# Low parts of weights, the sum of decay directions, the modulation and two copies of k and v placed on VectorE

## The chip, the cores and the metric

The kernel runs on one core of a Trainium2 chip. The metric is the device time of one launch in microseconds (us); the time of a kernel is the median of its runs. Engines are named as the profile names them: PE (TensorE, matrix products), VectorE (DVE), ScalarE (ACT), GpSimd (POOL) and SyncE (SP, which only issues DMAs here). SBUF is the memory on the core that the engines work in, PSUM the one that PE's results land in.

## The reference: what is computed

Two layers of a backbone, for 128 context tokens and 512 latent tokens that share every weight; the kernel holds them as five token tiles of 128 (tile 0 is the context). Each layer is one adaLN sub-layer:

```python
h = rms_norm(x, norm_w) * (1 + scale) + shift      # scale, shift, gate from silu(cond) @ mod_w
x = x + gate * mixer(h)
```

Layer 0's mixer is gated grouped-query attention (16 heads, 4 key/value heads, head width 64) with QK-norm and axial rotary positions; latent queries also see 128 cached keys. Layer 1's mixer is a bidirectional state-space scan (SSD: 32 heads in 4 groups, state 128, chunks of 128 tokens): a projection, a centred convolution of width 3 on x, B and C, a softplus for the time steps, and per group and chunk

```python
decay  = exp(a_cs[l] - a_cs[s]) below the diagonal (forward), above it (backward)
y_diag = ((c @ b.T) * decay) @ x
state  = state * chunk_decay + b.T @ (x * decay_end);   y_off = (c @ state) * exp(a_cs)
y      = rms_norm((y_forward + y_backward + d_skip * x) * silu(z)) @ w_out
```

All inputs and outputs are float32. The kernel returns both token streams, the new keys and values, and the final states of the context.

## The kernel before

**Split products.** PE multiplies in a shorter format. To keep float32 accuracy every operand is split in a high part (a cast) and a low part (the source less the high part), and each product is three: high x high, high x low, low x high. `split` (L72 to L74) does that: ScalarE casts (L73), and the engine given, VectorE unless another is named, subtracts (L74). For weights, `load_split` fetches a raw piece of up to 1024 columns by DMA into one of two buffers ("raw"), rotates the list `weng` by one and gives its first engine to `split`; "wh" and "wl" are the two halves of the result, in two buffers each. So `weng` says who makes the low parts of weights: GpSimd for the first key/value weights, VectorE for the rest of these and for the first q weights (L331, L336), GpSimd alone in the rest of layer 0 and at the start of layer 1 (L690, L1020), VectorE, GpSimd, GpSimd in turn from the fourth x unit of layer 1 on (L1234), VectorE alone from the output projection of layer 1 on (L1217).

**Layer 0.** The x tiles are normalised, transposed and modulated; keys and values of all five tiles are projected together in four quarters (`mm_kv`, L379), and after the last quarter ScalarE copies each tile's sum out of PSUM into `kv` (L396). A key chain per tile follows: sum of squares (L469, L472), `rstd` on GpSimd, scaling (L476), rotation (L487 to L490). Then come, per key/value head, q projections (L283), q chains of the same kind, scores (L630), softmax (L633, L637), transposed probabilities that are split (names pt, ph, pl), P times V (L668) and the silu gate (L527 to L530), while the modulation of layer 1 is projected in the background (L175). The output projection (L841) adds the gated result to x: VectorE multiplies (L865) and adds (L866) in quarters of 256 columns.

**Layer 1's input.** Each finished tile is normalised (L877, name xn), transposed by PE in two halves (L242), and `h_half` (L244 to L253) modulates each half, four blocks of 128 channels x 128 tokens: one VectorE multiplication by scale from PSUM with the scale spread over the tokens (L251), one GpSimd addition of shift (L252), then the split.

**Time steps and units.** A *unit* is a projection of 128 channels over all tokens (L914, 48 matmuls into one of two PSUM buffers "pj") and its evacuation: for x, B and C a convolution by three VectorE steps out of PSUM (L1001 to L1003), a ScalarE tanh (L1005) and one more step (L1006); for z a ScalarE tanh (L1068) and a VectorE step (L1069). The time-step stage (`dt_stage`) runs between the first x units: a chain of some twenty small VectorE steps on 128x320 (L947 to L962; L956 is a series of seven), then cumulative sums by three matmuls (L966, L967, L972), ScalarE exponentials and a store to device memory from which the decay tables are loaded.

**SSD groups.** For each of the four groups and five tiles: `a_load` fetches the two directions' cumulative sums, each spread over all partitions as 128x1024 (names am; the forward one in two buffers, the backward one in one); `decay` masks them on GpSimd (L1126, L1127), takes 16 exponentials on ScalarE (L1131) and adds the backward to the forward one on GpSimd (L1132), by which the only backward buffer comes free for the next tile's load; `mix` multiplies with C x B out of PSUM on VectorE (L1138); `diag` multiplies with x on PE (L1145). Besides, per group: states (L1192 on PE, L1195 and L1196 on VectorE), the off-diagonal part (L1186 to L1188), the gating of Y by silu(z) (L1097 on VectorE), and the units of the next group. Layer 1's output projection (L1383) takes its weights in pieces of 1024 columns.

**What sets the order.** The Python code gives the program; at build time a scheduler (`schedule_with_timeline_sim=True`, L1476) places every engine's instructions in an order of its own from estimates of their time. On the chip each engine works through its list in that order, so an instruction whose input is late holds all that stand behind it.

## Time and profile before

| | |
|---|---|
| three runs | 992.88, 988.27, 991.97 us |
| median | 991.97 us |
| profiled execution, its own time | 996.43 us |
| its span in the profile | 994.6 us |
| PE busy | 933.1 us, 94% of the span |
| VectorE, ScalarE, GpSimd busy | 663.8, 517.4, 411.8 us |
| mean granted TensorE clock | 0.979 of full speed |
| moved by DMA | 146.98 MB, mean 148 GB/s |

The profile is one execution. An engine is "busy" while it executes an instruction; time in which it waits for another engine or a DMA is idle time, put down to what ended it. Matmuls are pipelined, so a busy PE is not a PE at its peak. The stages follow one another: set-up and key/value stage to about 110 us, attention to 375, output projection of layer 0 with the normalisation of layer 1 to 460, time steps and first x units to 500, the four groups to 860, output projection of layer 1 to the end.

### The profile page before, as it was taken

What the parts mean: (1) busy time and instruction counts of PE and PEld (TensorE: products, weight loads), DVE (VectorE), ACT (ScalarE), POOL (GpSimd) and SP (SyncE); (2) the same over time, 40 slices, a digit from 0 to 9 for tenths busy, and PEclk for the clock granted to TensorE, in tenths of its full rate; (3) what the DMA queues carried; (4) which work ended last, traced back from release to release, by engine and by line L of the source; (5) the groups of instructions that cost most, each with busy time, mean ns of one, the idle gap of its engine ahead of it and who ended that gap; (6) DMA issues with size and microseconds to landing.
All of it is one profiled execution on the core that took longest, in us unless ns stands there. A gap on an engine that the chain in (4) does not pass through costs nothing.

```text
span 994.6 us, 17413 instructions
## 1 busy us (share of the span) xinstructions
PE 933.1 (94%) x6578; PEld 845.7 (85%) x6578; DVE 663.8 (67%) x1046; ACT 517.4 (52%) x1208; POOL 411.8 (41%) x397
## 2 busy tenths in 40 slices
PE   5998999999999989989899989999999999989898
PEld 3887979979997779989799979799889899768686
DVE  4468666566675774884858776856686657898553
ACT  5345666667675763333446565456436552544340
POOL 3245235227271071364235676448543862332000
PEclk9899999999999999999999999999999999999899
DMA  9941253131114223333449766755476545456742
GB/s 307 348 143 50 84 165 128 47 103 36 29 44 128 85 66 109 124 107 89 128 139 264 199 197 198 183 181 157 155 206 189 183 132 160 145 180 206 256 161 101
DMA packets 121476, 146.98 MB, mean 148 GB/s; under 512 B 8688, under 2 KB 93808, under 8 KB 121392
## 3 DMA queue, kind: packets, MB, share of 16 engines
q1 hardware_dynamic: 110640, 140.62, 46.0%
q10 hardware_dynamic: 10752, 5.24, 1.8%
q8 instruction: 52, 0.85, 0.4%
q14 instruction: 32, 0.26, 0.1%
HBM read 128.73 MB, written 17.10 MB: 147 GB/s over the span
## 4 chain that ended last, share of the span: by engine, by line
PE 55%; DVE 16%; DMA 12%; issue 6%; POOL 5%; ACT 5%; SPq 1%; ACTq 0%; POOLq 0%; DVEq 0%
PE pj L914 15%; PE pp L283 8%; DMA am<-acd 5%; PE pj L1383 3%; PE po L668 3%; PE acc L379 3%; PE a L841 3%; PE S L630 3%; PE pt L658 3%; DVE wl L74 2%; DMA u<-yzd 2%; PE pp L175 2%; PE a L1383 2%; POOL am L1132 2%; PE a L1192 2%
## 5 line engine op out<-in xcount | busy, mean ns | idle before, releaser
L914 PE MATMUL pj<-h,wh 128*128 128x322 f32 (+1 forms) x1248 | 289.9, 319 | 10.0 <-DVE B L1006 4.5
L914 PEld LDWEIGHTS pj<-h,wh 128*128 128x128 f32 (+1 forms) x1248 | 210.8, 189 | 19.2 <-issue 12.0
L74 POOL TENSOR_TENSOR wl<-raw,wh 128x512 fp32r<-128x512 f32 (+1 forms) x70 | 134.9, 1938 | 178.7 <-ACT wh L73 178.4
L914 PE MATMUL pj<-h,wl 128*128 128x322 f32 (+1 forms) x624 | 200.6, 322 | 0.0
L73 ACT CAST wh<-raw 128x1024 fp32r<-128x1024 f32 (+1 forms) x117 | 103.2, 912 | 91.3 <-DMA raw<-in_l_w_out 27.9
L1131 ACT ACTIVATE am<-am,nb 128x128 f32<-128x128 f32 x320 | 98.1, 390 | 57.6 <-POOL am L1127 46.2
L914 PEld LDWEIGHTS pj<-h,wl 128*128 128x128 f32 (+1 forms) x624 | 118.4, 190 | 4.2 <-issue 3.8
L283 PE MATMUL pp<-wh,big 128*128 128x256 f32 x576 | 112.2, 285 | 0.5 <-ACT sg L527 0.5
L74 DVE TENSOR_TENSOR wl<-raw,wh 128x1024 fp32r<-128x1024 f32 x47 | 66.7, 1428 | 40.9 <-ACT wh L73 40.9
L283 PEld LDWEIGHTS pp<-wh,big 128*128 128x128 f32 x576 | 91.2, 188 | 0.9 <-ACT sg L527 0.7
L283 PE MATMUL pp<-wl,big 128*128 128x256 f32 x288 | 81.2, 282 | 0.0
L74 DVE TENSOR_TENSOR pl<-pt,ph 128x512 fp32r<-128x512 f32 (+1 forms) x100 | 59.2, 599 | 25.6 <-ACT ph L73 25.0
L633 DVE TENSOR_REDUCE nm<-S 128x1 f32<-128x640 f32 x64 | 52.4, 820 | 13.7 <-PE S L630 12.7
L73 ACT CAST ph<-pt 128x512 fp32r<-128x512 f32 (+1 forms) x100 | 51.4, 518 | 18.8 <-PE pt L658 14.1
L1132 POOL TENSOR_TENSOR am<-am,am 128x1024 f32<-128x1024 f32 x20 | 49.2, 2458 | 22.5 <-ACT am L1131 22.5
L637 ACT ACTIVATE Pt<-S,nm 128x640 f32<-128x640 f32 x64 | 51.3, 803 | 13.1 <-PE pt L658 9.5
L1383 PE MATMUL pj<-wh,h 128*128 128x512 f32 x160 | 54.0, 412 | 2.1 <-ACT wh L73 2.1
L283 PEld LDWEIGHTS pp<-wl,big 128*128 128x128 f32 x288 | 54.3, 188 | 0.0
L630 PE MATMUL S<-kT,qT 128*128 128x320 f32 x256 | 51.4, 326 | 2.3 <-ACT Pt L637 2.3
L658 PE MATMUL pt<-cst,Pt 128*128 128x128 f32 x320 | 50.7, 275 | 2.7 <-DVE pl L74 2.3
L1126 POOL TENSOR_SCALAR_AFFINE_SELECT am<-am 128x1024 f32<-128x1024 f32 x20 | 23.5, 1176 | 59.0 <-DMA am<-acd 51.5
L841 PE MATMUL a<-wh,big 128*128 128x256 f32 x256 | 46.8, 283 | 0.0
(345 smaller groups left out, 2114.9 us busy)
## 6 DMA issues: line engine op xcount, KB each, us to landing
raw<-in_l_w_in SPq DMA_DIRECT2D x48, 512.0 KB
am<-acd SPq DMA_DIRECT2D x40, 512.0 KB
raw<-in_l_w_out SPq DMA_DIRECT2D x36, 512.0 KB
og<-in_l_mod_w SPq DMA_DIRECT2D x29, 512.0 KB
E<-ecd SPq DMA_DIRECT2D x64, 128.0 KB
raw<-in_l_w_in SPq DMA_DIRECT2D x25, 256.0 KB
mw<-in_l_mod_w SPq DMA_DIRECT2D x11, 512.0 KB
ys<-dud SPq DMA_DIRECT2D x20, 256.0 KB
```

The costliest lines, as they stand in the source:

```text
L73: (heng.tensor_copy if heng else self.nc.scalar.copy)(hi, src)
L74: (eng or self.nc.vector).tensor_tensor(lo, src, r32(hi), op=ALU.subtract)
L283: nc.tensor.matmul(ps, a[:, k, cs], b[:, k, :], start=k == 0 and a is hi and b is w[0], stop=k == KD - 1 and a is lo)
L630: nc.tensor.matmul(S[:, 192 + 320 * q:512 + 320 * q], qTs[g, t][:, h, :], kT[:, hl, 320 * q:320 * q + 320], start=hl == 0, stop=hl == 1)
L633: nc.vector.tensor_reduce(c["m"], c["s"], axis=AX.X, op=ALU.max, negate=True)
L637: nc.scalar.activation(Pt, c["s"], AF.Exp, bias=c["m"], scale=1.0, accum_out=rss[g][t][:, h:h + 1])
L658: nc.tensor.transpose(pt[:, 2 * i + j, :], Pts[j][:, kt * P:kt * P + P], self.ident)
L841: self.nc.tensor.matmul(ps, self.ohl[a][:, k, ts], w[b][:, k, :], start=k == 0 and i == 0, stop=k == KD - 1 and i == 2)
L914: nc.tensor.matmul(ps[0:m, 190 + 322 * half:512 + 322 * half], w[b][:, k, off:off + m], hT[s][:, k, 322 * half:322 * half + 322], start=fi ...
L1131: nc.scalar.activation(af[d][:, h, :], af[d][:, h, :], AF.Exp, bias=self.nb[:, t, i:i + 1], scale=1.0)
L1132: nc.gpsimd.tensor_tensor(af[0], af[0], af[1], op=ALU.add)
L1383: nc.tensor.matmul(self.PS[t][n], y[a][:, kk, :], b, start=k0 + k == 0 and i == 0, stop=k0 + k == 15 and i == 2)
```

## The change

Four edits put work on VectorE, and nothing that is computed changes.

1. The copies out of PSUM of k and v for the last two tiles (t of 3 and 4) are made by VectorE; the first three stay on ScalarE.
2. `weng` is VectorE alone in all the program but the first key/value weights. 66 low parts of weights (33 of 128x1024 and 33 of 128x512) go from GpSimd to VectorE; 4 at the start stay on GpSimd.
3. The sum of the two decay directions (20 of 128x1024) goes from GpSimd to VectorE.
4. In `h_half`, ten times, the multiplication of 128x512 on VectorE and the addition on GpSimd become four VectorE instructions of 128x128, each of which multiplies by scale and adds shift.

```diff
-        nc.vector.tensor_tensor(m, src, self.scale[layer][:, k, c:c + 1].to_broadcast([P, 4, P]), op=ALU.mult)
-        nc.gpsimd.tensor_tensor(m, m, self.shift[layer][:, k, c:c + 1].to_broadcast([P, 4, P]), op=ALU.add)
+        for i in range(4):
+            k_ = 4 * half + i
+            nc.vector.tensor_scalar(out=m[:, i, :], in0=src[:, i, :], scalar1=self.scale[layer][:, k_, c:c + 1], scalar2=self.shift[layer][:, k_, c:c + 1], op0=ALU.mult, op1=ALU.add)
         self.split(hi[:, k, cs], lo[:, k, cs], m)
...
-                        nc.scalar.copy(self.kv[:, :, 5 if t == 0 else t, :], acc[t].rearrange("p (a n) -> p a n", a=2))
+                        (nc.scalar.copy if t < 3 else nc.vector.tensor_copy)(self.kv[:, :, 5 if t == 0 else t, :], acc[t].rearrange("p (a n) -> p a n", a=2))
...
-        self.weng = [nc.gpsimd]
+        self.weng = [nc.vector]
         order = [1, 2, 0, 3, 4]
...
     def layer1(self, hT, wp, pj, pa, ctx):
...
-        self.weng = [nc.gpsimd]
         wk = self.pool("s2", bufs=2, ctx=ctx)
...
-            nc.gpsimd.tensor_tensor(af[0], af[0], af[1], op=ALU.add)
+            nc.vector.tensor_tensor(af[0], af[0], af[1], op=ALU.add)
...
     def part_mm(k0):
-            self.weng = [nc.vector]
...
-        self.weng = [nc.vector, nc.gpsimd, nc.gpsimd]
```

The first edit adds a line, so from there to about L1018 the changed kernel's line numbers are one higher than those of the kernel before (L915 for L914). Because the scheduler places all instructions anew, their order changes beyond the four edits. Three places follow; in each row stand the line, the operation, output<-inputs with the program's buffer numbers, and the shape.

The first is VectorE at the end of the key/value stage, before the change (qss and qn belong to the key chains, acc is the PSUM sum of one tile):

```order
L472 TENSOR_REDUCE qss_809<-qsq_803 128x4
L476 TENSOR_TENSOR qn_805<-kv_82,qss_799 128x256
L472 TENSOR_REDUCE qss_821<-qsq_813 128x4
L476 TENSOR_TENSOR qn_815<-kv_82,qss_809 128x256
L74 TENSOR_TENSOR wl_787<-raw_789,wh_788 128x1024
```

and after it:

```order
L473 TENSOR_REDUCE qss_809<-qsq_803 128x4
L477 TENSOR_TENSOR qn_805<-kv_82,qss_799 128x256
L397 COPY kv_82<-acc_105 128x2x256
L473 TENSOR_REDUCE qss_821<-qsq_813 128x4
L397 COPY kv_82<-acc_106 128x2x256
L477 TENSOR_TENSOR qn_815<-kv_82,qss_809 128x256
L74 TENSOR_TENSOR wl_787<-raw_789,wh_788 128x1024
```

The two copies stand among the key chains of earlier tiles and ahead of the next low part.

The second is VectorE in the time steps, before the change (am and xs are the chain's values, u_6307 is the evacuation of the second x unit, u_6399 that of the third):

```order
L1001 TENSOR_SCALAR u_6307<-pj_6308,cw_556,cols_110 128x641
L956 SCALAR_TENSOR_TENSOR am_1330_6153<-am_1330_6153 128x320
L1002 SCALAR_TENSOR_TENSOR u_6307<-pj_6308,cw_556,u_6307 128x641
L957 SCALAR_TENSOR_TENSOR am_1330_6153<-am_1330_6153,am_1329_6152 128x320
L1003 SCALAR_TENSOR_TENSOR u_6307<-pj_6308,cw_556,u_6307 128x641
L958 SCALAR_TENSOR_TENSOR am_1330_6153<-am_1329_6152,am_1330_6153 128x320
L960 SCALAR_TENSOR_TENSOR am_1331_6154<-am_1330_6153,xs_6150 128x320
L962 TENSOR_SCALAR am_1331_6154<-am_1330_6153 128x320
L1006 SCALAR_TENSOR_TENSOR u_6307<-pj_6308,u_6307 128x641
```

and after it, where the second x unit is u_6327 and the third u_6419:

```order
L957 SCALAR_TENSOR_TENSOR am_1330_6173<-am_1330_6173 128x320 x2
L1007 SCALAR_TENSOR_TENSOR u_6327<-pj_6328,u_6327 128x641
L957 SCALAR_TENSOR_TENSOR am_1330_6173<-am_1330_6173 128x320
L1002 TENSOR_SCALAR u_6419<-pj_6420,cw_556,cols_110 128x641
...
L957 SCALAR_TENSOR_TENSOR am_1330_6173<-am_1330_6173 128x320 x2
L1007 SCALAR_TENSOR_TENSOR u_6419<-pj_6420,u_6419 128x641
L958 SCALAR_TENSOR_TENSOR am_1330_6173<-am_1330_6173,am_1329_6172 128x320
L959 SCALAR_TENSOR_TENSOR am_1330_6173<-am_1329_6172,am_1330_6173 128x320
L961 SCALAR_TENSOR_TENSOR am_1331_6174<-am_1330_6173,xs_6170 128x320
```

The chain's last steps stood inside the second unit's evacuation; now they stand behind the third's. On PE, the cumulative sums stood before the change inside the third unit (pj_6400):

```order
L914 MATMUL pj_6400<-h_1183_5264,wl_6389 128x322
L966 MATMUL a_6374<-am_1331_6154,xs_6150 128x5x32
L967 MATMUL a_6374<-am_1331_6154,xs_6150 128x5x32
L972 MATMUL a_6379<-am_1331_6154,xs_6150 128x320
L914 MATMUL pj_6400<-h_1183_5264,wh_6390 128x322
```

and after it behind that unit's last matmul (pj_6420):

```order
L915 MATMUL pj_6420<-h_1183_5264,wl_6409 128x322
L967 MATMUL a_6394<-am_1331_6174,xs_6170 128x5x32
L968 MATMUL a_6394<-am_1331_6174,xs_6170 128x5x32
L973 MATMUL a_6399<-am_1331_6174,xs_6170 128x320
L1015 MATMUL a_6474<-cst_60,u_6327 128x128 x4
L1015 MATMUL a_6480<-cst_60,u_6327 128x128
L983 MATMUL pj_6486<-cst_60,am_1331_6174 64x128 x5
```

They moved by three matmuls, to a place where no matmul of that unit is left behind them.

The third is VectorE at the end of the first SSD group, before the change (B_1503 is the evacuation of the C unit of the next group, zs that of a z unit, ys the gating of Y):

```order
L1002 SCALAR_TENSOR_TENSOR B_1503_7484<-pj_7485,cw_556,B_1503_7484 128x641
L74 TENSOR_TENSOR wl_7740<-raw_7746,wh_7741 128x1024
L1097 TENSOR_TENSOR ys_6023<-ys_6023,zs_6034 128x4x128
L1097 TENSOR_TENSOR ys_6023<-ys_6023,zs_6035 128x4x128
L1003 SCALAR_TENSOR_TENSOR B_1503_7484<-pj_7485,cw_556,B_1503_7484 128x641
L1006 SCALAR_TENSOR_TENSOR B_1503_7484<-pj_7485,B_1503_7484 128x641
L1069 SCALAR_TENSOR_TENSOR zs_7549<-zs_7549,pj_7550 128x642
```

and after it (am is the sum of the decay directions, of the next group's first two tiles):

```order
L1007 SCALAR_TENSOR_TENSOR B_1497_7432<-pj_7433,B_1497_7432 128x641
L1097 TENSOR_TENSOR ys_6043<-ys_6043,zs_6054 128x4x128
L1097 TENSOR_TENSOR ys_6043<-ys_6043,zs_6055 128x4x128
L1132 TENSOR_TENSOR am_1519_7699<-am_1519_7699,am_1520_7700 128x1024
L1007 SCALAR_TENSOR_TENSOR B_1503_7504<-pj_7505,B_1503_7504 128x641
L1132 TENSOR_TENSOR am_1525_7745<-am_1525_7745,am_1526_7746 128x1024
L1069 SCALAR_TENSOR_TENSOR zs_7569<-zs_7569,pj_7570 128x642
```

Two sums now stand on VectorE, one ahead of the last step of the C unit's evacuation and one ahead of the z unit's.

## Rows read from the trace of the kernel before

**Rows 1.** Page: busy us (share of the span) x instructions, by engine.

```profile
PE 933.1 (94%) x6578; PEld 845.7 (85%) x6578; DVE 663.8 (67%) x1046; ACT 517.4 (52%) x1208; POOL 411.8 (41%) x397
```

**Rows 2.** Busy us by stretch: window, length, engines (x instructions), PE clock, DMA, GB/s.

```profile
110.00:375.00 265.00, 255.53 (x1986) 228.10 (x1979) 175.17 (x374) 176.63 (x438) 103.73 (x142) 0.99 0.26 83
375.00:460.00 85.00, 81.48 (x629) 79.56 (x629) 56.05 (x89) 29.75 (x81) 32.24 (x29) 0.98 0.31 102
460.00:500.00 40.00, 35.34 (x239) 33.98 (x238) 26.52 (x35) 16.76 (x26) 14.58 (x6) 1.00 0.38 111
500.00:860.00 360.00, 345.36 (x2427) 324.10 (x2426) 248.68 (x288) 188.51 (x459) 196.17 (x130) 0.98 0.64 183
860.00:995.00 135.00, 123.05 (x556) 98.61 (x554) 90.46 (x110) 50.17 (x77) 22.09 (x26) 0.96 0.52 174
```

**Rows 3.** PE's waits, whole span: line <- releaser: total us, times, longest.

```profile
PE pj L914 <- DVE B L1006: 4.5, 3, 2.0
...
PE pj L914 <- ACT Wh L984: 2.4, 1, 2.4
...
PE pt L658 <- DVE pl L74: 2.3, 5, 0.7
...
PE S L283 <- ACT kv L396: 2.3, 1, 2.3
PE a L1014 <- DVE u L1006: 2.3, 1, 2.3
```

**Rows 4.** GpSimd by line and shape: count, busy us, mean ns, idle before, its releaser.

```profile
L74 POOL TENSOR_TENSOR wl<-raw,wh 128x1024 fp32r<-128x1024 f32 x33 | 85.6, 2607 | 72.4 <-ACT wh L73 72.4
...
L1132 POOL TENSOR_TENSOR am<-am,am 128x1024 f32<-128x1024 f32 x20 | 49.2, 2458 | 22.5 <-ACT am L1131 22.5
```

**Rows 5.** VectorE by line and shape, columns as in rows 4.

```profile
L74 DVE TENSOR_TENSOR wl<-raw,wh 128x1024 fp32r<-128x1024 f32 x47 | 66.7, 1428 | 40.9 <-ACT wh L73 40.9
...
L74 DVE TENSOR_TENSOR pl<-pt,ph 128x512 fp32r<-128x512 f32 x68 | 45.9, 684 | 13.4 <-ACT ph L73 12.8
...
L1138 DVE TENSOR_TENSOR am<-am,a 128x1024 f32<-128x1024 f32 x20 | 24.3, 1215 | 31.9 <-POOL am L1132 22.8 <-PE a L1137 9.1
L1097 DVE TENSOR_TENSOR ys<-ys,zs 128x512 f32<-128x512 f32 x12 | 22.2, 1863 | 0.2
...
L370 DVE TENSOR_SCALAR hm<-x,scale,shift 128x128 f32<-128x128 f32 x8 | 3.7, 458 | 0.1
...
L617 DVE TENSOR_TENSOR og<-pt,o 128x128 f32<-128x128 f32 x8 | 2.2, 287 | 2.0 <-PE pt L562 1.6
```

**Rows 6.** In order of time, VectorE and GpSimd, 433 to 447: start, us, instruction.

```profile
433.89 5.14 POOL L74 TENSOR_TENSOR wl<-raw,wh 128x1024 fp32r<-128x1024 f32 x2
433.96 2.85 DVE L877 TENSOR_SCALAR xn<-y,ss 128x1024 f32<-128x1024 f32 x1 [0.39 <-POOL ss L90]
...
436.74 2.58 DVE L866 TENSOR_TENSOR y<-y,om 128x256 f32<-128x256 f32 x1
...
446.05 0.75 DVE L877 TENSOR_SCALAR xn<-y,ss 128x1024 f32<-128x1024 f32 x1 [0.44 <-POOL ss L90]
```

**Rows 7.** In order of time, key/value stage: ScalarE's last copy, VectorE's rope products.

```profile
67.44 0.58 ACT L396 COPY kv<-acc 128x512 f32<-128x512 f32 x1
...
86.11 2.57 DVE L487 TENSOR_TENSOR qsq<-qn,tabq 128x128 f32<-128x128 f32 x2
```

**Rows 8.** Pieces of the chain that ended last, in order of time: start, us, what.

```profile
475.10 0.86 DVE u L1001
...
478.78 0.49 DVE am L956
...
589.86 4.31 DVE ys L1097 x2
...
696.81 2.63 DVE wl L74
```

**Rows 9.** The forward mask's instructions: duration in ns, min/median/max, start times, form.

```profile
L1126 POOL TENSOR_SCALAR_AFFINE_SELECT am<-am x20: 1084/1094/2075, 518.5 to 863.3; 128x1024 f32<-128x1024 f32 x20
```

## The prediction

> **What bounds the kernel now.** The page's first line comes first: PE is busy 933.1 of the 994.6 us span, VectorE 663.8, GpSimd 411.8 [rows 1]. PE is the bound, so a change elsewhere is worth what it does to PE's gaps and to nothing else. Next the busy times by stage [rows 2]: from 110 to 375 us (attention) PE stands idle for 9.5 of 265 us, from 375 to 460 (output projection of layer 0, normalisation of layer 1) for 3.5 of 85, from 460 to 500 (time steps) for 4.7 of 40, from 500 to 860 (the four SSD groups) for 14.6 of 360, after that for 12.0 of 135. [...] Then PE's waits [rows 3]: few and short, mostly for a VectorE result.
>
> Last, what makes those VectorE results late. Operations with two SBUF inputs have a mean far above their size: the gating of Y takes 1863 ns for 128x512, while a low part of that size with a PSUM input takes 684, and 128x1024 low parts from SBUF take 1428 against 1215 for the PSUM-fed multiplication of 128x1024 [rows 5]. Twelve gatings and 47 low parts alone lose 12 x 1.18 + 47 x 0.21 = 24 us to this; over all such operations, each against the shortest of its own shape, I count some 78, about 66 of them beside GpSimd operations that the change moves. The order of time shows why: at 433.89 GpSimd starts two low parts that end at 439.03; VectorE's normalisation, started at 433.96, takes 2.85 us (0.75 for the next tile), and the 128x256 addition behind it 2.58 us, until 439.3 [rows 6]; its size lies between 128x128 and 128x512, which take 0.29 and 0.68 from PSUM [rows 5], so some 0.4 alone. So an operation of that kind stands still until GpSimd's is over. GpSimd's low part takes 2607 ns and its sum of directions 2458 [rows 4]; both are long holders, and both are what the change moves.
>
> **The change part by part.** The sum is made against the profiled execution, 996.43 us, 0.45% above the median of 991.97; differences are carried over in microseconds.
>
> Copies of k and v. PE's last kv matmul ends at 65.8, and the next projection waits 2.3 us for ScalarE's last copy [rows 3], which sits at 67.44 to 68.02 behind two weight casts of 1.05 [rows 7]. On VectorE both stand among short operations; a 128x512 operation from PSUM takes 0.68 [rows 5], so one begun at 65.8 ends at 66.5. Gain 1.5, between 0 (the following key chain is the limit) and 2.3.
>
> Norms of q and k. Two rope products (L487) of 128x128 stand 2.57 us [rows 7] under GpSimd's two low parts; at 0.29 each, as another product of that size [rows 5], they would take 0.6. The low parts are now two VectorE operations of 0.68 each [rows 5]. 2.0 back, 1.4 spent, but the latter beside waits for the projection: gain 1, between 0 and 2.5.
>
> Attention. 28 low parts of 128x512 come onto VectorE, 28 x 0.684 = 19 us [rows 5] on an engine with 175 busy of 265 us. Cover: PE hardly waits for VectorE's 68 similar splits of the probabilities [rows 5]; the largest such row is 2.3 us in 5 waits [rows 3]. At 2.3/68 to three times that per split, 28 more cost 0.9 to 2.8 us; I take a loss of 2. Ends: a gain of 4 (locks vanish) and a loss of 8 (half of the 19 us uncovered).
>
> Modulation and layer 0's output. Each half tile was one VectorE multiplication of 0.68 us plus a GpSimd addition; it becomes four VectorE pieces. No row shows a 128x128 scale-and-shift out of PSUM. The same step out of SBUF takes 458 ns, a 128x128 product out of PSUM 287 [rows 5]: 4 x 0.29 = 1.15 us to 4 x 0.46 = 1.83. I take the former, for the source; that is 0.5 more per half on VectorE, but one handoff and GpSimd's addition fewer in the chain. [...] Of the locked 2.85 and 2.58 us [rows 6], 0.75 (the next tile's) and 0.4 stay: 4.3 back, two low parts (2.4) and 1.3 of pieces spent; and that norm, for which PE waited, now comes ahead of the low parts. Gain 2, between 0 and 4.5.
>
> Time steps: a loss. Before, the time-step chain (L947 to L960; one more in the changed kernel's lines, which the next two sentences use) ran ahead of the second x unit's evacuation, and PE covered it with the third unit. Now, by the order, the third unit's whole evacuation (u_6419) stands on VectorE before L958 to L961, and PE has L967 directly behind that unit's matmuls. PE must wait for all of it: eight VectorE steps like those from 475.10 to 480.01, 4.91 us, and three like the last but one of these, 0.49 each [rows 8]: 6.4 together, plus 0.75 since VectorE also carries two 1.2 us low parts meanwhile: some 7.2. The two waits of before, 2.3 and 2.4 [rows 3], go, since the first unit is evacuated under the second one's matmuls. Net loss 2.5, between a gain of 4.7 and a loss of 3.5.
>
> SSD groups. Five waits lead back to moved or locked work: the diagonal product at 585 (one sum of directions 1.2 us shorter), the B unit at 596 (two gatings in 4.31 us, 1.3 unlocked, and PE waits 1.9), the scan at 631 (a locked gating, 1.8), the B unit at 700 (a low part in 2.63 us, 1.2 unlocked, and a sum of 2.9 on GpSimd; 2.2), the z unit at 786 (a low part in 2.75; 2.3). 9.4 together, as the chain of waits has them (its first and last piece stand in [rows 8]), and 3 of the 7 us of low clock behind them. Against it: VectorE gets 21 low parts and 18 sums, 39 x 1.22 = 48 us, and gets back some 28 of the 66 of lock, so its load rises from 249 to about 268 of 360 us; I put 3 us of new waits on that, a fifth of the rise. And a sum must wait for the exponentials of its tile: GpSimd stood 22.5 us for them [rows 4]. Now VectorE stands in that wait, and what is queued behind it is, by the order, the last step of the next C unit (named B in the rows, as is the B unit) and that of a z unit, for which PE waits. I let a seventh through, 3.4. Gain 6, between 21 (every idle and slow us) and a loss of 13.
>
> Tail, after 860: low parts were on VectorE already, only two sums move, and two operations of some 2.5 us lose their lock. Gain 1.5, between 0 and 4.
>
> Sum: -1.5 - 1 + 2 - 2 + 2.5 - 6 - 1.5 = -7.5. Profiled 988.9; as a median 992.0 - 7.5 = **984.5 us**.
>
> **The rivals.** *Nothing to measure* (within 0.5%, 987.0 to 996.9): the freed VectorE time is off PE's path, the moved work costs what the lock gave back, and attention or the time steps take the rest. For it: PE is busy 94%, and VectorE's busy sum rises by some 28 us even after the lock (33 x 1.22 + 33 x 0.68 + 20 x 1.22 of low parts and sums, 6 of pieces and copies, less 66). With the groups at -1 instead of -6 it gives 989.5.
>
> *Slower, by head-of-line waits*: the sums of the next group's first two tiles now stand ahead of the B and z evacuations. It decides where the exponentials end later than the evacuation was ready, at a group's end about 596 and 607 us. If the whole 22.5 us comes through instead of 3.4, the sum is -7.5 + 19.1 = +11.6: 1003.6. For it: loads of 6 us stand between two sums in the chain. Against: each sum now frees its buffer 1.2 us sooner.
>
> *The lock turns round*: VectorE's new operations have two SBUF inputs themselves and may hold up what is left on GpSimd, the masks and the weighting of x in the groups. Those show it little today: of 20 masks the median takes 1094 ns, the shortest 1084, the longest 2075 [rows 9]. If four of the 40 masks lost 1 us, as the longest did, it would cost 4 us of the decay chain, half of it seen by PE: 986.5. [...]
>
> *Much faster*: all idle and slow time of the groups goes, -21 instead of -6: 969.5.
>
> **How the numbers follow.** Forecast (972 to 987) 0.50, nothing 0.23, slower by head-of-line 0.13, lock turned round 0.06 (around 986.5, half on either side of the bound), much faster 0.08. A measurement tells about 0.5% from no change. Faster by more: 0.50 + 0.03 + 0.08 = 0.61; within: 0.23 + 0.03 = 0.26; slower: 0.13. The range 972 to 997 leaves out the much faster case and most of the slower one, 0.18 together. Its upper end also holds the bounds of attention (+6) and of the groups with the rest as taken.
>
> **What the changed profile would show.** VectorE some 692 us busy, GpSimd 223; means of 128x1024 low parts near 1.22 and of the gating below 0.9; no wait at the kv projection, a single PE wait of about 7 us before the cumulative-sum matmuls (L967) in place of two; in the groups no PE wait for B evacuations except behind a sum. Wrong would be: locked operations unchanged (then GpSimd's low parts were not the holders), PE waits in attention growing past 8 us, or VectorE idle before the sums by 20 us with PE waiting behind it.

## The result and the profile after

The changed kernel took 1006.3 us in the median of its runs, the kernel before 990.1 (the three runs above and a fourth of 988.16): a ratio of 1.0131, interval 1.0097 to 1.0166. It is slower by 1.3%, where 984.5 us, faster than before, was forecast, and it lies outside the range of 972 to 997. The profiled execution of the changed kernel ("after" in what follows) took 1005.27 us; its span is 1003.5. In two of the experiments below, launches of 1492 to 3123 us occurred (two of four in e1, one of six in e12); they are left out of every median and ratio.

The first line of the page, busy time by engine, answers to [rows 1]:

```profile
PE 932.7 (93%) x6578; PEld 847.0 (84%) x6578; DVE 686.8 (68%) x1164; ACT 515.0 (51%) x1206; POOL 239.2 (24%) x301
```

PE is as busy as before, so the whole difference is in its gaps. VectorE's 686.8 us (forecast 692) and GpSimd's 239.2 (forecast 223) say that the work moved as described.

To see where the gaps are, both spans are cut at the same five matmuls: the last matmul of the key/value stage, the first of layer 0's output projection behind attention (96 of its products run earlier, among the heads) and its last, the first of layer 1's units, the first product of C and B in the first group. The rows give window, length, then busy time of PE, PEld, DVE, ACT, POOL (instructions), PE clock, DMA share, GB/s. Before:

```profile
0.00:65.52 65.52, 53.41 (x443) 45.38 (x444) 30.81 (x70) 30.29 (x67) 18.28 (x31) 0.95 0.87 286
65.52:383.86 318.34, 303.30 (x2365) 272.59 (x2364) 215.88 (x465) 206.88 (x519) 128.41 (x176) 0.99 0.26 83
383.86:434.22 50.36, 49.98 (x415) 49.36 (x413) 36.11 (x62) 18.23 (x50) 20.07 (x19) 1.00 0.32 112
434.22:448.45 14.23, 11.11 (x67) 10.43 (x66) 11.92 (x13) 3.23 (x9) 9.73 (x7) 0.88 0.46 136
448.45:523.86 75.41, 70.75 (x482) 69.04 (x483) 43.58 (x57) 33.02 (x61) 25.92 (x17) 1.00 0.40 120
523.86:990.02 466.16, 444.54 (x2815) 398.86 (x2813) 324.11 (x380) 225.73 (x507) 208.67 (x149) 0.97 0.61 181
```

and after:

```profile
0.00:62.98 62.98, 51.39 (x443) 44.10 (x444) 31.12 (x71) 29.84 (x66) 18.20 (x31) 0.97 0.89 298
62.98:385.73 322.75, 303.47 (x2363) 271.89 (x2362) 225.96 (x496) 204.78 (x516) 91.03 (x144) 0.99 0.26 81
385.73:437.42 51.69, 51.69 (x415) 51.33 (x416) 35.52 (x86) 19.49 (x53) 3.08 (x8) 0.97 0.33 113
437.42:451.70 14.28, 11.23 (x68) 10.51 (x66) 11.51 (x26) 3.02 (x7) 1.04 (x2) 0.88 0.53 153
451.70:530.85 79.15, 72.52 (x482) 70.69 (x483) 45.70 (x67) 32.12 (x57) 7.20 (x8) 0.96 0.36 107
530.85:998.85 468.00, 442.45 (x2815) 398.47 (x2813) 335.58 (x420) 225.78 (x511) 118.00 (x109) 0.98 0.59 181
```

Attention is 4.4 us longer, the output projection 1.3 (at a clock of 0.97 instead of 1.00), the time steps 3.7, groups and tail 1.8. The first stretch is 2.5 shorter, but that is no gain of the change: it lasted 62.4 to 63.9 in every profile of the thirteen experiments below, with and without each part, so 65.5 was a chance of the one profile of before. The same holds for the last stretch: e3 below, which has before's order from 456 us on, measured 461.5 there, and against that after's groups and tail lose 6.5. Cut further at the first product of C and B in the second group, the loss lies in the first group: it lasts 95.8 us after, and 87.2 to 87.6 in the three profiles with before's order there (before, e3 and e11). All that follows takes 372.2 against 372.6 to 378.9.

PE's waits after, which answer to [rows 3] (us in total, times, longest):

```profile
PE pj L915 <- DVE B L1007: 11.4, 4, 5.2
PE a L967 <- DVE am L961: 6.6, 1, 6.6
...
PE pj L915 <- DVE u L1007: 5.1, 3, 3.7
...
PE a L842 <- DVE og L686: 1.5, 1, 1.5
...
PE S L284 <- DVE kv L397: 0.9, 1, 0.9
```

The wait for the last step of a B or C unit grew from 4.5 to 11.4 us, that of the same kind for x units from 0.3 to 5.1, the single wait in the time steps is there, and the one behind the copies of k and v fell from 2.3 to 0.9.

VectorE by line and shape after, which answers to [rows 5] (count, busy us, mean ns, idle time before and its releaser):

```profile
L74 DVE TENSOR_TENSOR wl<-raw,wh 128x1024 fp32r<-128x1024 f32 x80 | 99.9, 1258 | 43.9 <-ACT wh L73 43.9
...
L1132 DVE TENSOR_TENSOR am<-am,am 128x1024 f32<-128x1024 f32 x20 | 27.1, 1354 | 28.0 <-ACT am L1131 25.8 <-issue 2.2
...
L253 DVE TENSOR_SCALAR hm<-pj,scale,shift 128x128 f32<-128x128 f32 x40 | 13.4, 402 | 2.0 <-PE pj L242 2.0
...
L1097 DVE TENSOR_TENSOR ys<-ys,zs 128x512 f32<-128x512 f32 x12 | 10.4, 874 | 0.2
```

The gating fell from 1863 to 874 ns, low parts of 128x1024 from 1428 to 1258. Counted as in the prediction, the stretch of VectorE's operations fell from 78 to 21 us. So the lock was real, and taking GpSimd's long operations away did undo it. But the second row holds what it cost: VectorE stood idle for 28.0 us ahead of the sums, 25.8 of them for ScalarE's exponentials. Before, it was GpSimd that stood 22.5 us in that place [rows 4].

One such place, in order of time, VectorE, ScalarE and GpSimd after, where PE waits 3.7 us for the last x unit of the second group, which is evacuated while the first group runs (start, us, instruction, idle time before it and its releaser):

```profile
574.90 0.88 DVE L1004 SCALAR_TENSOR_TENSOR u<-pj,cw,u 128x641 f32<-128x641 f32 x1
...
576.35 1.09 POOL L1126 TENSOR_SCALAR_AFFINE_SELECT am<-am 128x1024 f32<-128x1024 f32 x1 [8.32 <-DMA am<-acd]
577.47 2.44 ACT L1131 ACTIVATE am<-am,nb 128x128 f32<-128x128 f32 x8 [2.41 <-POOL am L1126]
578.44 0.70 DVE L1187 TENSOR_TENSOR a<-a,E 128x512 f32<-128x512 f32 x1 [2.66 <-ACT am L1131]
579.82 0.69 ACT L1006 ACTIVATE pj<-u 128x641 f32<-128x641 f32 x1
579.94 1.09 POOL L1126 TENSOR_SCALAR_AFFINE_SELECT am<-am 128x1024 f32<-128x1024 f32 x1 [2.50 <-DMA am<-acd]
580.01 2.10 DVE L1132 TENSOR_TENSOR am<-am,am 128x1024 f32<-128x1024 f32 x1 [0.87 <-ACT am L1131]
...
582.03 0.67 DVE L1188 TENSOR_TENSOR ys<-ys,a 128x512 f32<-128x512 f32 x1
582.63 0.69 DVE L1187 TENSOR_TENSOR a<-a,E 128x512 f32<-128x512 f32 x1
583.23 0.81 DVE L1007 SCALAR_TENSOR_TENSOR u<-pj,u 128x641 f32<-128x641 f32 x1
```

The third convolution step ends at 575.8. The tanh could follow, but on ScalarE it stands behind eight exponentials (577.47), which wait for a mask, which waits for a load. The tanh ends at 580.5. On VectorE the unit's last step now stands behind a sum, which waits for the same exponentials and lasts 2.10 us. So the step ends at 584.0; directly behind the tanh it would have ended at about 581.3. PE waits for it.

### The profile page after: what moved, and what is told of

Its sections match the earlier page's. It is cut to its first block, busy times and chain, and to the rows that moved or that the text cites. A ratio compares the mean times of both kernels' runs of the same rounds, so it can differ in the third digit from the quotient of the medians.

```text
span 1003.5 us, 17456 instructions
## 1 busy us (share of the span) xinstructions
PE 932.7 (93%) x6578; PEld 847.0 (84%) x6578; DVE 686.8 (68%) x1164; ACT 515.0 (51%) x1206; POOL 239.2 (24%) x301
## 4 chain that ended last, share of the span: by engine, by line
PE 63%; DVE 13%; DMA 10%; ACT 6%; issue 4%; POOL 3%; SPq 0%; ACTq 0%; DVEq 0%; POOLq 0%
PE pj L915 18%; PE pp L284 8%; PE pj L1381 6%; DMA am<-acd 6%; PE a L842 4%; PE po L669 3%; PE acc L380 3%; ACT am L1131 3%; PE S L631 3%; PE pt L659 3%; DVE wl L74 2%; PE pp L175 2%; PE a L1381 2%; PE a L1084 2%; PE a L1186 1%
## 5 line engine op out<-in xcount | busy, mean ns | idle before, releaser
L915 PE MATMUL pj<-h,wh 128*128 128x322 f32 (+1 forms) x1248 | 291.3, 320 | 18.6 <-DVE B L1007 11.4
L915 PEld LDWEIGHTS pj<-h,wh 128*128 128x128 f32 (+1 forms) x1248 | 212.4, 191 | 28.5 <-issue 12.9
L915 PE MATMUL pj<-h,wl 128*128 128x322 f32 (+1 forms) x624 | 201.2, 322 | 0.0
L74 DVE TENSOR_TENSOR wl<-raw,wh 128x1024 fp32r<-128x1024 f32 (+1 forms) x113 | 123.7, 1105 | 49.6 <-ACT wh L73 49.3
L915 PEld LDWEIGHTS pj<-h,wl 128*128 128x128 f32 (+1 forms) x624 | 119.1, 191 | 3.7 <-issue 3.5
L1157 POOL TENSOR_TENSOR xw<-xt,ws 128x512 f32<-128x512 f32 x32 | 39.2, 1244 | 106.2 <-DMA acd<-Wh 61.6
L842 PE MATMUL a<-wh,big 128*128 128x256 f32 x256 | 48.6, 289 | 1.5 <-DVE og L686 1.5
L659 PEld LDWEIGHTS pt<-cst,Pt 128*128 128x128 f32 x320 | 37.4, 142 | 10.6 <-PE S L631 5.0
L1132 DVE TENSOR_TENSOR am<-am,am 128x1024 f32<-128x1024 f32 x20 | 27.1, 1354 | 28.0 <-ACT am L1131 25.8
```

The lines of the kernel that those rows point to most:

```text
L74: (eng or self.nc.vector).tensor_tensor(lo, src, r32(hi), op=ALU.subtract)
L659: nc.tensor.transpose(pt[:, 2 * i + j, :], Pts[j][:, kt * P:kt * P + P], self.ident)
L842: self.nc.tensor.matmul(ps, self.ohl[a][:, k, ts], w[b][:, k, :], start=k == 0 and i == 0, stop=k == KD - 1 and i == 2)
L915: nc.tensor.matmul(ps[0:m, 190 + 322 * half:512 + 322 * half], w[b][:, k, off:off + m], hT[s][:, k, 322 * half:322 * half + 322], start=fi ...
L1157: nc.gpsimd.tensor_tensor(h3(xw), h3(xts[g][:, t, :]), bch(self.ws[:, t, sl(g, d)]), op=ALU.mult)
```

## The experiments

Each ratio is against runs of the kernel before that were taken together with it (medians 990.7 for e1 to e4, 993.0 for e5 to e7, 993.4 for e8 to e11, 994.3 for e12 and e13). The last four columns are the lengths of the stretches cut as above, in us, each from one profile.

| | in the kernel | median us | ratio (interval) | attention | output proj. | time steps | groups, tail |
|---|---|---|---|---|---|---|---|
| before | | 990.1 | 1 | 318.3 | 50.4 | 75.4 | 466.2 |
| after | all four parts | 1006.3 | 1.0131 (1.0097 to 1.0166) | 322.7 | 51.7 | 79.1 | 468.0 |
| e1 | sums | 999.6 | 1.009 | 319.1 | 50.4 | 76.0 | 469.7 |
| e2 | low parts | 990.7 | 0.9987 (0.9956 to 1.0019) | 320.1 | 50.1 | 79.4 | 458.5 |
| e3 | modulation | 991.8 | 1.0008 (0.9980 to 1.0036) | 319.0 | 50.4 | 76.0 | 461.5 |
| e4 | all but sums | 998.8 | 1.0070 (1.0040 to 1.0100) | 323.2 | 51.7 | 79.2 | 461.5 |
| e5 | low parts from group 2 on | 988.9 | 0.9935 (0.9914 to 0.9956) | 318.2 | 50.4 | 75.7 | 459.3 |
| e6 | low parts, modulation | 990.8 | 0.9980 (0.9950 to 1.0009) | 319.1 | 50.1 | 78.6 | 462.3 |
| e7 | low parts, copies | 995.1 | 1.0017 (0.9987 to 1.0046) | 323.1 | 51.7 | 79.5 | 457.1 |
| e8 | sums of tiles 2 to 4 | 993.2 | 0.9998 (0.9968 to 1.0028) | 319.3 | 50.4 | 76.0 | 464.0 |
| e9 | sums of tiles 1 and 5 | 997.8 | 1.0054 (1.0028 to 1.0081) | 320.3 | 50.4 | 76.5 | 467.3 |
| e10 | low parts in groups 2, 3 | 986.3 | 0.9924 (0.9894 to 0.9954) | 319.1 | 50.4 | 76.0 | 461.7 |
| e11 | copies | 992.8 | 0.9985 (0.9960 to 1.0010) | 322.5 | 50.4 | 76.3 | 459.9 |
| e12 | all but copies | 1000.0 | 1.0055 (1.0018 to 1.0092) | 320.3 | 50.1 | 79.5 | 466.1 |
| e13 | e10, sums 2 to 4 of group 4 | 988.0 | 0.9955 (0.9932 to 0.9977) | 319.2 | 50.4 | 76.1 | 458.3 |

e1's ratio, 999.6 by 990.7, rests on two runs (999.55 and 999.68) and has no interval. The stretches need care: before, e3 and e11, which share one order in the first three groups, differ by up to 6 us in the last column.

**One part at a time: e1 to e4.** The sums alone:

```diff
-            nc.gpsimd.tensor_tensor(af[0], af[0], af[1], op=ALU.add)
+            nc.vector.tensor_tensor(af[0], af[0], af[1], op=ALU.add)
```

> The kernel before with one part of the change: the 20 sums of the decay directions on VectorE, all low parts of weights still where they were. Theory S (sums): in the changed kernel VectorE idles 25.8 us in 8 waits before a sum (L1132) for ScalarE's exponentials, and evacuations stand behind them, so this part alone costs the groups most of the loss seen there: 996 to 1000 us against 990 of before, with PE waits for the last step of a unit (L1006) of 8 us or more in all. Theory L (low parts): the sums are harmless, since the engine is not crowded without the low parts: 988 to 992.

e2 is before with the edits of `weng` alone, e3 with the modulation alone:

> The kernel before with one part of the change: all low parts of weights on VectorE, sums and modulation as before. In its order the time-step matmuls stand behind the third unit's last matmul as in the changed kernel, so both theories expect one PE wait of 6 to 7 us there (a net 3 to 4 us), and VectorE's means of locked operations to fall (gating below 1.2 us for 128x512). Theory S: the rest gains a few us in the groups, 988 to 994 in all. Theory L: 33 us more on VectorE delay the evacuations, PE waits for L1006 of 8 us or more, 999 to 1004.

> The kernel before with the modulation alone changed to four VectorE instructions of 128x128 per half. Both theories: within 2 us of before (988 to 992); the pieces take about 0.40 us each as in the changed kernel, and the time-step matmuls stand inside the third unit as before.

e4 is the changed kernel with

```diff
-            nc.vector.tensor_tensor(af[0], af[0], af[1], op=ALU.add)
+            nc.gpsimd.tensor_tensor(af[0], af[0], af[1], op=ALU.add)
```

> The changed kernel with the 20 sums back on GpSimd. Theory S: the groups lose their waits, 994 to 998 (what is left is the time steps, 3.7 us, and attention with the output projection, some 5). Theory L: hardly better than the changed kernel, 1003 to 1007. Both: VectorE operations beside a sum on GpSimd are stretched again (about 11 us of the 78 before).

The sums alone cost 9 us, as theory S has it, and the low parts alone nothing, against theory L (e2 lies in theory S's range). In e2 the lock is gone (gating, now L1096, 837 ns) and the time-step wait is there; rows of VectorE by shape and of PE's waits:

```profile
L1096 DVE TENSOR_TENSOR ys<-ys,zs 128x512 f32<-128x512 f32 x12 | 9.8, 837 | 0.3
```

```profile
PE a L966 <- DVE am L960: 6.9, 1, 6.9
```

e4 came out just above theory S's range: 6 us better than the changed kernel, but 8 worse than the low parts alone, which neither theory had. With the modulation alone at 1.0008, that pointed to the copies or to a pair.

In e1 the same pattern as in after stands at the first group's end. VectorE there before the change, then ScalarE, VectorE and PE in e1, in order of time:

```profile
577.78 0.95 DVE L1001 TENSOR_SCALAR B<-pj,cw,cols 128x641 f32<-128x641 f32 x1 [0.22 <-PE a L1137]
...
584.88 0.82 DVE L1006 SCALAR_TENSOR_TENSOR B<-pj,B 128x641 f32<-128x641 f32 x1
```

```profile
578.95 2.46 ACT L1131 ACTIVATE am<-am,nb 128x128 f32<-128x128 f32 x8 [4.90 <-POOL am L1127]
...
581.49 1.23 DVE L1132 TENSOR_TENSOR am<-am,am 128x1024 f32<-128x1024 f32 x1 [3.29 <-ACT am L1131]
...
582.63 0.94 DVE L1001 TENSOR_SCALAR B<-pj,cw,cols 128x641 f32<-128x641 f32 x1
...
586.70 2.15 ACT L1131 ACTIVATE am<-am,nb 128x128 f32<-128x128 f32 x7 [2.32 <-POOL am L1126]
...
588.76 0.69 ACT L1005 ACTIVATE pj<-B 128x641 f32<-128x641 f32 x1
...
589.50 0.82 DVE L1006 SCALAR_TENSOR_TENSOR B<-pj,B 128x641 f32<-128x641 f32 x1
...
590.37 0.90 PE L914 MATMUL pj<-h,wh 128*128 128x322 f32 x2 [4.47 <-DVE B L1006]
```

VectorE stands 3.29 us before the fifth tile's sum, and the B unit's first step only comes behind it, at 582.63; before the change it ran at 577.78, while GpSimd stood 2.64 us in that wait. Its tanh then stands behind seven more exponentials, its last step ends 4.6 us later than before, and PE waits 4.47.

**Which sums: e8 and e9.** The sums by their place j in a group's five tiles:

```diff
-            nc.gpsimd.tensor_tensor(af[0], af[0], af[1], op=ALU.add)
+            (nc.vector if [0, 2, 3, 1, 4].index(t) in (1, 2, 3) else nc.gpsimd).tensor_tensor(af[0], af[0], af[1], op=ALU.add)
```

and (0, 4) in place of (1, 2, 3) for e9.

> The kernel before with 12 of the 20 sums on VectorE: those of the second, third and fourth tile of each group; the first and the fifth tile's stay on GpSimd. Theory H (the sums cost by what stands behind them: at a group's end, where the first and the fifth tile's sums stand ahead of the B, C and z evacuations): 989 to 993 against 990 to 993 of before, since the middle tiles' sums stand among work with more slack. Theory P (every sum costs alike, by its 1.2 us and its wait): 12 of 20, that is some 5 us more than before, 995 to 998.

> The complement: the 8 sums of each group's first and fifth tile on VectorE, the other 12 on GpSimd. Theory H: nearly the whole loss of the sums, 997 to 1000, with PE waits for the last step of the B and C units at a group's end. Theory P: 8 of 20, some 3 us more than before, 993 to 996.

The twelve middle sums cost nothing (0.9998), the eight at a group's ends 0.54%, which is some 5 of e1's 9 us. Theory P asked for 5 and 3 us, in the other order. VectorE by shape, e8 first, then e9:

```profile
L1132 DVE TENSOR_TENSOR am<-am,am 128x1024 f32<-128x1024 f32 x12 | 20.4, 1697 | 18.1 <-ACT am L1131 10.7 <-issue 4.4 <-POOL wl L74 2.9
```

```profile
L1132 DVE TENSOR_TENSOR am<-am,am 128x1024 f32<-128x1024 f32 x8 | 11.7, 1458 | 10.0 <-ACT am L1131 7.5 <-POOL wl L74 2.5
```

VectorE waited longer before the harmless ones (10.7 us for exponentials) than before the costly ones (7.5). So the length of the wait does not set the cost. What is queued behind it in e9 is, at the first group's end, the B unit's second step; VectorE, then PE:

```profile
576.53 0.95 DVE L1001 TENSOR_SCALAR B<-pj,cw,cols 128x641 f32<-128x641 f32 x1 [0.20 <-PE a L1137]
580.62 1.23 DVE L1132 TENSOR_TENSOR am<-am,am 128x1024 f32<-128x1024 f32 x1 [3.15 <-ACT am L1131]
581.77 0.88 DVE L1002 SCALAR_TENSOR_TENSOR B<-pj,cw,B 128x641 f32<-128x641 f32 x1
...
589.06 0.82 DVE L1006 SCALAR_TENSOR_TENSOR B<-pj,B 128x641 f32<-128x641 f32 x1
```

```profile
589.94 0.91 PE L914 MATMUL pj<-h,wh 128*128 128x322 f32 x2 [4.97 <-DVE B L1006]
```

That the place decides, as theory H has it, is shown by the two medians and not by the profiles. In the four groups PE waits 7.9 us for units' last steps in e8 (none above 1.7) and 6.7 in e9 (one of 5.0); the first three groups take 305.5 and 303.3 us; only from the fourth group on is e8 the shorter one, 158.6 against 163.9. Nor is a middle sum harmless in every order: the one in the example from after is the first group's fourth.

**The pair: e6, e7, e11, e12.** Before with the edits of the low parts and the modulation (e6), the low parts and the copies (e7), the copies alone (e11); after without the copies (e12):

> The kernel before with the low parts and the modulation changed, copies and sums as before. Low parts alone measured 990.7, the modulation alone 991.8, both with the copies 998.8: 7 us are in a pair. Theory M (the four pieces, 0.40 us each where one multiplication took 0.68, hurt only where VectorE also has the low parts): 996 to 1000, with the output projection and the norms some 4 us longer than with low parts alone. Theory K (the two copies): 989 to 993.

> The kernel before with the low parts and the two copies of k and v changed, modulation and sums as before. Theory M: 989 to 993. Theory K: the copies move the order of attention, 995 to 999, with attention 1 to 2 us longer than with low parts alone and the rest in the groups.

> The kernel before with only the last two copies of k and v on VectorE. The wait of the next projection for ScalarE's copy (2.4 us) should fall to about 1. With the low parts, the copies added some 3 us in attention and 1.6 in the output projection by another order of the heads' work. Theory O (that is the order of the pair): alone they give 987 to 991. Theory K (the copies' own): 994 to 997.

> The changed kernel with the last two copies of k and v back on ScalarE. Alone the copies moved nothing (992.8 against 993.4); with the low parts they lengthened attention by 3 us and the output projection by 1.6 by another order of the heads' work. Theory O (the pair's order costs, in the changed kernel too): attention and output projection shrink by 4 to 5 us together, 999 to 1003 against 1006.3. Rival (the sums and low parts carry it all): 1004 to 1008.

The modulation is not it: e6 measures as e2. The copies are in it by their place: in all four kernels with them attention lasts 322.5 to 323.2 us, in all eleven without 318.2 to 320.3, although the wait that they were to shorten is shorter. With the low parts the output projection lasts 51.7 instead of 50.1 besides. Without the copies the changed kernel's attention falls to 320.3, its output projection to 50.1, and its ratio from 1.0131 to 1.0055, as theory O has it for e12. As a total the copies' cost shows only together: alone they measure 0.9985, and e7's interval holds both no change and theory K's lower end, so the price of the low parts and the copies alone is unclear.

Four of the kernels have the low parts and the modulation and differ only in sums and copies: e6 has neither (0.9980), e12 the sums (1.0055), e4 the copies (1.0070), the changed kernel both (1.0131). So the sums cost some 7.5 us without the copies and 6 with them, the copies some 9 without the sums and 7.5 with them, and the two together make up the whole loss. With the sums, PE's waits for units' last steps grow from 0.3 us in e6 to 13.7 in e12:

```profile
PE pj L915 <- DVE B L1007: 0.3, 1, 0.3
```

```profile
PE pj L915 <- DVE B L1007: 8.9, 4, 3.7
...
PE a L1015 <- DVE u L1007: 4.8, 4, 3.9
```

and from 8.8 in e4 to 17.2 in the changed kernel (11.4 and 5.1 above, and 0.7 of the second kind here). In e4 they are:

```profile
PE pj L915 <- DVE B L1007: 4.4, 4, 1.8
PE a L1015 <- DVE u L1007: 4.4, 2, 2.4
```

The changed kernel's two longest waits for a B unit, 5.2 and 4.5 us, fall at the ends of the first and third group, each with the fifth tile's sum ahead of the unit on VectorE.

What the copies do there is a change of order. In e11 nothing else was edited, and two waits of PE in the first heads grew, the first from 0.9 us in 2 waits, the second from nothing:

```profile
PE pt L550 <- DVE pl L74: 2.8, 3, 1.9
...
PE pp L283 <- ACT ev L447: 1.2, 1, 1.2
```

PE's order in e11 differs from before's only up to 163 us and again from 860 on, and its 3.5 us against e3 are lost within the first 800 products of attention. In the kernels with low parts and copies the loss has another place: attention's 2000th product starts 264.9 to 265.3 us after the last of the key/value stage, and 264.1 to 265.9 in those with the low parts and without the copies (e2, e6, e12); some 3 us are lost behind that, in the last heads. There the output projection begins with a tile whose gated head VectorE has just finished; that is the row of 1.5 us for L842 above. The granted clock of the stretch behind it is 0.97 in these three kernels (after, e4, e7), and 1.00 in e2, e6 and e12.

**A better place for the low parts: e5, e10, e13.** VectorE from the second group on (e5); only in the second and third group (e10, the second form):

```diff
         for g in range(NG):
             last = g == NG - 1
+            if g == 1:
+                self.weng = [nc.vector]
...
+            if g:
+                self.weng = [nc.vector, nc.gpsimd, nc.gpsimd] if last else [nc.vector]
```

e13 is e10 with the fourth group's second to fourth sum on VectorE.

> The kernel before, with VectorE making all low parts from the second SSD group on, and GpSimd as before up to there; sums, modulation and copies as before. Its order is that of the kernel before up to the end of the first group, so time steps, attention and first group cost what they did. With low parts alone the second and third group took 98.3 and 99.4 us in their profile against 105.1 and 108.5 before, while the first took 94.1 against 87.2 and the time steps 79.4 against 75.4. Theory U (the gain of the unlocked groups is real, the loss is the place): 974 to 982. Theory D (the later groups only catch up what the first one delayed): 987 to 992.

> The kernel before with VectorE making all low parts during the second and third group only; the fourth group's pieces go to VectorE, GpSimd, GpSimd in turn as before. With VectorE from the second group to the end, the groups' part after the third took 168.0 us against 165.0 and 162.3 in two profiles with the order of before. Theory U: this returns to 162 to 165, so 984 to 987, the fastest so far. Rival: the last stretch is paid for by what comes before it, 988 to 991.

> Low parts on VectorE in the second and third group only, as in the run that measured 0.9924 of before, and besides the sums of the three middle tiles of the fourth group on VectorE. With the middle tiles' sums of all groups on VectorE, the stretch from the fourth group to the end took 158.2 us in its profile, where 162 to 165 were seen otherwise. Theory H (a sum is harmless where no evacuation that PE waits for stands behind it, and worth the lock it takes away): 981 to 985, 0.987 to 0.990 of before. Rival (that stretch was a chance of one profile): 985 to 988.

e5 and e10 are faster than before, by 0.65% and 0.76%, and so faster than the changed kernel. The two are not told apart. The time steps keep before's order. The first group keeps it up to about 586 us and still lasts 92.3 and 91.8 us in their profiles, where before's order shows 87.2 to 87.6. The second group gains: 97.5 and 97.9 against 101.1 to 105.1. For the third group the cut misleads: PE's products in it are 746 before and in e10, but 697 in e2 and e5, because one unit's 48 products have moved behind the cut. So the 99.4 us against 108.5 in e5's expectation is not a gain of that size, and the 168.0 against 165.0 in e10's is not a loss. Third group and rest together took 269.4 in e5 and 272.0 in e10, against 271.4 to 273.8 with before's order. So a gain is located in the second group only; e10's profile is of a run of 991.1 us, 5 above its median, and can't show more.

Theory U had its sign; its size for e5 (974 to 982) was too much, since it was read from a profile of before that was 5 us long in the groups and from that cut of the third group. e5's 988.9 lies in theory D's range, but before was slower beside it (993.0 instead of 990.7). e13 is not better than e10, and from its fourth group on it took 163.0 us, not e8's 158.6 (158.2 in the expectation). So that a sum with nothing urgent behind it gains isn't shown, nor whether e8's short stretch was a chance of one profile.

## Why the prediction was wrong, point by point

- **What bounds the kernel; the lock: right.** VectorE's stretched time fell from 78 to 21 us, and the means came out near those named (low parts 1.26, gating 0.87).
- **Copies of k and v: the wait right, the sign of the term wrong.** The wait fell from 2.3 to 0.9 us. But where a gain of 1.5 us was put, the copies cost 7.5 in the changed kernel (1.0131 against 1.0055 in e12), and attention is 2 to 5 us longer in every kernel with them. The step that failed is that the copies were costed where they stand, and the order that they change further on was not looked at.
- **Norms of q and k: right in kind.** The rope products' mean fell from 546 to 286 ns; no run measures the term by itself.
- **Attention: a loss of 2 from the low parts, not seen.** With them and without the copies it lasts 320.1, 319.1 and 320.3 us (e2, e6, e12), against 318.2 to 320.3 in the eight kernels with neither; a loss of about 1 would be hidden in that spread. (Half of the 19 us is 9.5, not the bound of 8.)
- **Modulation and layer 0's output: about zero instead of a gain of 2.** A piece takes 402 ns, not the 287 taken, and lies between the two bounds: 1.61 us a half instead of 1.15. The 458 behind the upper bound was no price of the step alone: seven of its eight took 335 to 351 ns, and one of 1248 lifted the mean. From the output projection's end to the first unit, the stretch was 14.2 before, 11.8 with the low parts alone, 13.0 with the modulation too (e6), 14.3 after.
- **Time steps: right in mechanism.** One PE wait of 6.6 us where 7.2 was said; net 3.7 in place of 2.5. e2, e4, e6, e7 and e12 have it, e1, e3, e5, e8 to e11 and e13 don't, so it goes with the low parts made before the second group. Before the change the chain's last steps stood inside the second unit's evacuation and not, as the prediction has it, ahead of it; that doesn't touch the sum.
- **SSD groups: a loss instead of a gain of 6; beside the copies, the step that decided.** The mis-sized term is the sums': "I let a seventh through, 3.4" of 22.5 us. The wait was 25.8 us, and the sums cost 9 us alone (two runs), 7.5 beside low parts and modulation (e12 against e6) and 6 in the changed kernel (1.0131 against 1.0070). I had read from the order that the C and z units' last steps stand behind the first two sums of the next group. I had not seen that the fifth tile's sum stands ahead of the B unit too, nor that on ScalarE the units' tanh stands behind the same exponentials, so that one late load holds GpSimd, ScalarE and VectorE one after the other (8.32, 2.41 and 0.87 us in the example from after), and PE behind them (3.7). The prediction's own sign of being wrong came: VectorE stood 28.0 us before the sums, with PE waiting behind it. No run shows the 3 us of low clock in the term (of 7, which is 0.02 of 360 us [rows 2]): between 500 and 860 us before, and between 507 and 867 after, slices of 1 us go down to a clock of 0.50, and what they lack of the full clock adds up to 6.8 us in both. The low parts' term is not settled by the profiles, 458.5 alone (e2) against 459.9 to 466.2 with before's order; as a total the low parts gain 0.76% where only the second and third group have them (e10). The tail's gain of 1.5 can't be read either: from the fourth group on PE has 826 products after and 778 before, in 166.5 us against 162.6 to 165.4. The range was also too narrow by the prediction's own numbers: it says that its upper end holds the groups' bound, but a loss of 13 there in place of the gain of 6 gives 1003.5, not 997.
- **The lock turned round: there, and small.** The mean of the weighting of x on GpSimd rose from 1131 to 1244 ns: two of them at 746.26 took 3.10 us, two at 842.59 took 2.04, and a sum of 1.21 us on VectorE had begun at 747.24, just ahead of the second. The means of the two masks rose by 20 and 41 ns only. In the old direction the lock is still there: the sum at 580.01 took 2.10 us behind a mask that had begun 0.07 us before. In both rows the one that began later lasted about the rest of the other and its own time: 2.10 us for that sum, with 1.02 of the mask left and a median of 1.23 for a sum; 2.10 for the second weighting, with 1.2 of the sum left and a median of 1.04 for a weighting.
- **The rival that came true** is *slower, by head-of-line waits*, at 1003.6 with a chance of 0.13. Its mechanism is shown by e1 and by the pairs e6 and e12, e4 and after. Its price, all 22.5 us, isn't what happened, and that 1003.6 lies near 1006.3 is luck: of the 16 us some 6 to 7.5 are the sums and 7.5 to 9 the copies. The time steps' loss is real, but the low parts that cause it come out at nothing in total (e2 0.9987, e6 0.9980).

What stays open: the low parts with the copies measure 1.0017, with the modulation 0.9980, with both 1.0070 (e4). The 5 us more of both have no single place in the profiles (1 in the norms, the rest in the groups, where profiles with one and the same order differ as much). Why the order of the heads is worse with the copies was not tried, and why the sums' place in a group matters as much as e8 and e9 say, the profiles don't show.

## What to carry to other kernels

When a step moves to another engine, its duration is not all that moves: the wait in front of the sums moved along (22.5 us on GpSimd before, 25.8 on VectorE after), and on VectorE it became the wait of what stood behind them (3.29 us ahead of the B unit's first step in e1). So look, before moving, at who releases the step and at what the new engine has queued after it: here sums with 10.7 us of such waits were free in the middle of the groups, and sums with 7.5 us cost 5 at their ends. Where a scheduler places the instructions, try each part of a change alone and in the stretches where it pays; here one piece of the change (low parts in two groups) beat both kernels, and two copies that were harmless alone cost 7 to 9 us beside the other parts.

## What the runs showed of the hardware that was not expected

A VectorE scale-and-shift of 128x128 with two operands per partition took 396 to 411 ns out of PSUM (all 40 in after), and 335 to 351 out of SBUF (seven of eight before), while a product of two 128x128 operands, one of them in PSUM, took 280 to 292 (all eight before). So here a scale-and-shift of a quarter of 128x512 took 0.59 of the product of the whole that it replaced (0.402 of 0.682 us), not a quarter.
